# Sums of weight quarters in a down projection: by VectorE, or by DMAs that add in SBUF

## The chip, the cores and the metric

The kernel runs on one core of one Trainium2 chip. The metric is the device time of one execution in microseconds; the times shown are of several runs, and one further execution was recorded by the hardware profiler. Its instructions, DMAs and waits make the trace, and times in the trace count from its first instruction.

## The reference

One layer of a diffusion backbone: modulated input, one combined projection for two groups of attention heads, attention, output projection with gated residual and layer norm, and then the part that matters here, a gated feed-forward network with the same residual rule. All arrays are float32.

```python
SEQ = 256; D_MODEL = 2048; FFN_HIDDEN = 5632
def swiglu(u, w_gate, w_up, w_down):
    return (jax.nn.silu(u @ w_gate) * (u @ w_up)) @ w_down
...
x = layer_norm(DN_ALPHA * x + g2 * swiglu(modulate(x, sh2, sc2), w_gate, w_up, w_down), ln2_g, ln2_b)
```

The down projection is the last product: 256 tokens by 5632 hidden values, times a 5632 x 2048 weight.

## The kernel before, in words

Float32 accuracy is made of three products. Every operand is split in two: `hi` is the value rounded to the matmul's format (a cast on ScalarE, L236 or L230) and `lo` is what is left (a subtraction on VectorE, L237 or L231). `mm3` (L239 and the lines after it) then issues three matmuls for one 128 x 512 tile, hi by hi (L240), hi by lo (L241) and lo by hi (L242).

Weights are loaded by SP's queue (L208) as 1 MB tiles called `raw`, in four buffers. A buffer goes to a later load as soon as all that reads or writes it is done. The split parts lie in tiles `hi` and `lo` of 128 x 1024, four buffers of each, used in turn: the fifth split waits until TensorE is done with the first.

**The down projection.** The hidden dimension is cut into 11 blocks f of 512, the output columns into 4 groups n of 512, and groups are done in pairs (n, n + 1) by `pair`. There are two kinds of blocks:

- Eight whole blocks, `plain`. Each is loaded and split once per column group: f0 to f7 for group n, s0 to s7 for group n + 1 in what follows. One such step loads 1 MB, makes two splits and issues 24 matmuls (2 halves of the tokens, 4 slices of 128 hidden values, 3 matmuls).
- Three blocks with half products, `by_quarters`, for f = 8, 9, 10. They do both column groups at once by a scheme of seven half products in place of eight. The weight of 512 x 1024 is taken as quarters b11, b12 (in the first load, `r1`) and b21, b22 (in the second, `r2`); the activations likewise, with sums s1 to s4 made by `quarter_sums`. The seven products are called b, p1, a, p7, p5, p6 and c; each has one split and 6 matmuls. Four of them need sums of weight quarters. These are four subtractions or additions of 128 x 1024 on VectorE (L1759), between the splits; two go in place, into `raw`, and two into the tile `sums`.

**What sets the order.** The call order is written by `ORDER`: f0 f1 8 f2 f3 9 f4 f5 f6 10 f7, then s0 to s7. A block with half products stands there as one piece: two loads, seven splits with the four sums between them, 42 matmuls. The scheduler then arranges each engine's list by readiness; TensorE keeps the call order. `turn()` counts calls and starts, at fixed counts, the steps that turn the last hidden block's activations and build the sums of blocks 8 to 10. After the products of a pair `combine_parts` and `first_block` add them up, gate them and add them to the residual; `l2_loads` (two 1 MB loads on SP) and `rows_of_last_norm` (two fills and twelve small DMAs on GpSimd) prepare the last norm.

GpSimd has nothing else to do in the down projection.

Of the kernel before, what the change touches and what calls it, by code (L numbers as in the profile page):

```python
# [163 lines left out]
def dit_layer(ctx: ExitStack, tc: tile.TileContext, x, c, cx, c_ctx, w_ada, b_ada, w_in, q_norm_g,  # L164
# [1573 lines left out]
    def by_quarters(f, n, bank, begins, ends):  # L1738
        r1, r2 = (load_raw(w_down, f * 4 + k, 2, n * NB, 2 * NB).rearrange("p (k n) -> p k n", k=2) for k in (0, 2))
        (b11, b12), (b21, b22) = ([r[:, :, :NB], r[:, :, NB:]] for r in (r1, r2))  # L1740
        x1, x2 = (room["x"][:, i].rearrange("p (k n) -> p k n", k=2) for i in range(2))
        h = [(c[f][:, 0:2, :P], c[f][:, 2:4, :P], c[f][:, 2:4, P:]) for c in (hTh, hTl)]
        q = quarters[f]
        lefts = {n: [h[c][i] for c in range(2)] for i, n in enumerate(("a11", "a12", "a22"))}
        lefts.update({f"s{i + 1}": [q[c][:, i] for c in range(2)] for i in range(4)})
        sub, add = ALU.subtract, ALU.add
        for name, left, right, after in (
            ("p1", "a11", b11, (x1, b22, b12, sub)),
            ("b", "s4", b22, (b12, b12, b11, sub)),
            ("a", "a12", b21, (x2, x1, b11, add)),  # L1750
            ("p7", "s3", x1, (b21, b21, x2, sub)),
            ("p5", "s1", b12, None),
            ("p6", "s2", x2, None),
            ("c", "a22", b21, None),
        ):
            hi, lo = (whl.tile([P, SUB * NB], F32R, tag=tag, name=tag).rearrange("p (k n) -> p k n", k=2) for tag in ("hi", "lo"))
            split(hi, lo, right)
            if after:
                nc.vector.tensor_tensor(after[0], after[1], after[2], op=after[3])  # L1759
# [182 lines left out]
```

## Time and profile before

| What | Value |
|---|---|
| Median of 3 runs | 1115.16 us (1114.07 to 1115.31) |
| Profiled execution, its own time | 1115.46 us |
| Its span, first to last instruction | 1113.6 us |
| TensorE busy (modelled ends) | 1100.1 us |
| VectorE busy | 899.3 us |
| Granted clock of TensorE, mean | 0.997 |
| First matmul of the down projection | at 870.23 us |
| Its last | at 1102.76 us |

In the profile PE is TensorE's matmuls and PEld its weight loads, DVE is VectorE, ACT ScalarE, POOL GpSimd, SP the engine that issues most DMAs; SPq is its queue. A row of the order of time has start, duration, engine, line, operation, operands, and in brackets how long the engine stood idle before it and who ended that. Since matmuls overlap, the distance from one start to the next says how fast TensorE goes, not the 0.39 us of each.

### The profile page before, as it was taken

Reading aid. Unit: us, or ns where it says so; the run is one execution under the profiler, and the core shown is the slowest. Engines: PE = TensorE matmul, PEld = TensorE weight load, DVE = VectorE, ACT = ScalarE, POOL = GpSimd, SP = SyncE. Lnnn points to the kernel's source line nnn. Section 1 sums busy time; section 2 is a strip of 40 time slices with the busy share of each in tenths; the row PEclk is TensorE's granted clock in tenths of the full one; section 3 lists DMA queues with packets and bytes.
Section 4 is the critical chain, followed back from the end, with each engine's and each line's share of the span. In section 5 each row is a group of like instructions: output and inputs, shape, how many; then the busy total and the mean of one; then the engine's idle time right before and its main releaser. Section 6 shows DMA issues by size and latency. Waiting matters only on the chain.

```text
span 1113.6 us, 13934 instructions
## 1 busy us (share of the span) xinstructions
PE 1100.1 (99%) x5138; PEld 888.5 (80%) x5138; DVE 899.3 (81%) x1082; ACT 603.6 (54%) x870; POOL 48.5 (4%) x100
## 2 busy tenths in 40 slices
PE   8999999999999999999999999999999999999997
PEld 6677788778878788888888888888888788888886
DVE  2469999999989898877666776887875899678895
ACT  3345675786765356444465455655654565346550
POOL 1000050102000010000000000000000000001000
PEclk9999999999999999999999999999999999999999
DMA  9999998889999789989757898898896576546661
GB/s 344 374 401 393 396 337 323 300 274 312 328 317 366 278 314 359 336 288 346 269 207 279 288 323 286 304 309 306 310 317 216 164 249 226 192 151 224 222 236 76
DMA packets 175658, 321.28 MB, mean 288 GB/s; under 512 B 9283, under 2 KB 47075, under 8 KB 173285
## 3 DMA queue, kind: packets, MB, share of 16 engines
q1 hardware_dynamic: 173718, 319.23, 81.3%
q10 hardware_dynamic: 1264, 1.11, 0.3%
q8 instruction: 40, 0.66, 0.2%
q14 instruction: 28, 0.23, 0.1%
q0 software_dynamic: 608, 0.06, 0.0%
HBM read 304.11 MB, written 16.25 MB: 288 GB/s over the span
## 4 chain that ended last, share of the span: by engine, by line
PE 92%; DMA 3%; DVE 3%; ACT 1%; issue 0%; SPq 0%; ACTq 0%; DVEq 0%
PE acc L240 22%; PE acc L242 22%; PE acc L241 22%; PE wk L242 7%; PE wk L241 7%; PE wk L240 7%; PE wk L558 2%; PE wk L1036 2%; DMA raw<-in_w_ada_dram 2%; DVE adav L359 1%; DMA pT<-pd 1%; PE wk L728 1%; DMA adav<-in_b_ada_dram 0%; DVE lo L237 0%; DMA pd<-hx 0%
## 5 line engine op out<-in xcount | busy, mean ns | idle before, releaser
L231 DVE TENSOR_TENSOR lo<-raw,hi 128x1024 fp32r<-128x1024 f32 x232 | 280.9, 1221 | 126.8 <-ACT hi L230 124.0
L230 ACT CAST hi<-raw 128x1024 fp32r<-128x1024 f32 x232 | 244.0, 1056 | 245.3 <-PE acc L242 140.1
L240 PE MATMUL acc<-hi,u2h 128*128 128x512 f32 x448 | 175.1, 391 | 0.0
L242 PE MATMUL acc<-hi,u2l 128*128 128x512 f32 x448 | 174.6, 390 | 0.2 <-DVE u2l L1574 0.2
L241 PE MATMUL acc<-lo,u2h 128*128 128x512 f32 x448 | 174.5, 389 | 0.0
L359 DVE SCALAR_TENSOR_TENSOR adav<-raw,cs,adav 128x1024 f32<-128x1024 f32 (+1 forms) x96 | 114.4, 1191 | 6.1 <-DMA raw<-in_w_ada_dram 2.9
L507 ACT CAST hi<-raw 128x1024 fp32r<-128x1024 f32 x84 | 87.7, 1052 | 55.9 <-PE acc L242 28.7
L510 DVE TENSOR_TENSOR lo<-raw,hi 128x1024 fp32r<-128x1024 f32 x84 | 101.2, 1220 | 9.9 <-ACT hi L507 9.7
L240 PE MATMUL acc<-hi,hTh 128*128 128x512 f32 x264 | 102.6, 389 | 0.6 <-ACT hi L236 0.6
L240 PE MATMUL acc<-hi,uh 128*128 128x512 f32 x256 | 102.8, 402 | 0.3 <-ACT uh L741 0.3
L241 PE MATMUL acc<-lo,hTh 128*128 128x512 f32 x264 | 102.7, 389 | 0.0
L242 PE MATMUL acc<-hi,hTl 128*128 128x512 f32 x264 | 102.5, 389 | 0.0
L242 PE MATMUL acc<-hi,ul 128*128 128x512 f32 x256 | 100.3, 392 | 0.0
L241 PE MATMUL acc<-lo,uh 128*128 128x512 f32 x256 | 99.8, 390 | 0.0
L242 PE MATMUL wk<-hi,u2l 128*128 128x512 f32 x256 | 99.6, 389 | 0.0
L241 PE MATMUL wk<-lo,u2h 128*128 128x512 f32 x256 | 99.6, 389 | 0.0
L240 PE MATMUL wk<-hi,u2h 128*128 128x512 f32 x256 | 99.6, 389 | 0.0
L240 PEld LDWEIGHTS acc<-hi,u2h 128*128 128x128 f32 x448 | 84.1, 188 | 18.1 <-ACT u2h L1573 0.8
L242 PEld LDWEIGHTS acc<-hi,u2l 128*128 128x128 f32 x448 | 84.1, 188 | 18.1 <-DVE u2l L1574 0.6
L241 PEld LDWEIGHTS acc<-lo,u2h 128*128 128x128 f32 x448 | 84.1, 188 | 17.7 <-DVE lo L231 0.4
L240 PEld LDWEIGHTS acc<-hi,uh 128*128 128x128 f32 x256 | 48.1, 188 | 16.1 <-ACT acc L522 2.5
L240 PEld LDWEIGHTS acc<-hi,hTh 128*128 128x128 f32 x264 | 49.6, 188 | 11.4 <-ACT hi L236 1.0
(328 smaller groups left out, 1753.2 us busy)
## 6 DMA issues: line engine op xcount, KB each, us to landing
raw<-in_w_ada_dram SPq DMA_DIRECT2D x64, 1024.0 KB, 7.3
raw<-in_w_gate_dram SPq DMA_DIRECT2D x44, 1024.0 KB, 6.0
raw<-in_w_up_dram SPq DMA_DIRECT2D x44, 1024.0 KB, 5.7
raw<-in_w_down_dram SPq DMA_DIRECT2D x44, 1024.0 KB, 5.9
raw<-in_w_ada_dram SPq DMA_DIRECT2D x64, 512.0 KB, 6.3
raw<-in_w_in_dram SPq DMA_DIRECT2D x18, 1024.0 KB, 8.5
raw<-in_w_out_dram SPq DMA_DIRECT2D x16, 1024.0 KB, 6.4
pd<-hx SPq DMA_DIRECT2D x64, 128.0 KB, 4.7
```

The costliest lines, as they stand in the source:

```text
L230: nc.scalar.copy(hi[:, :n], raw[:, s : s + n])
L231: nc.vector.tensor_tensor(lo[:, :n], raw[:, s : s + n], hi[:, :n].bitcast(F32), op=ALU.subtract)
L240: nc.tensor.matmul(ps, lhsT=xh, rhs=w[0], start=first, stop=False, skip_group_check=seeded)
L241: nc.tensor.matmul(ps, lhsT=xh, rhs=w[1], start=False, stop=False, skip_group_check=seeded)
L242: nc.tensor.matmul(ps, lhsT=xl, rhs=w[0], start=False, stop=last, skip_group_check=seeded)
L359: nc.vector.scalar_tensor_tensor(a[:, c : c + piece], raw[:, f : f + piece], cs[:, 4 * (g * (G4 * NB // w) + j) + 2, None], a[:, c : c + p ...
L507: nc.scalar.copy(hl.hi[:, :n], raw.t[:, s : s + n])
L510: nc.vector.tensor_tensor(hl.lo[:, :n], raw.t[:, s : s + n], hl.hi[:, :n].bitcast(F32), op=ALU.subtract)
L558: nc.tensor.matmul(bank.t[32 * j : 32 * j + 32, :width], lhsT=cs[:, 4 * k + 2 - 2 * i : 4 * k + 34 - 2 * i], rhs=raw.t[:, c * width : (c + ...
L728: nc.tensor.transpose(ps.t[:, (j * 2 + t) * P : (j * 2 + t + 1) * P], src, ident)
L1036: nc.tensor.matmul(o_ps.t[:, : 2 * P].rearrange("p (g q) -> p g q", q=32), lhsT=v, rhs=pv[:, k], start=k == 0, stop=k == 3)
```

## The change

The four sums of weight quarters are made by DMAs that add: GpSimd issues a DMA from one quarter to another, in SBUF, with an addition at the destination (`put_on`). There is only an addition, so the signs are turned: quarters add up where they were subtracted, the activation sums s1 to s4 are subtracted the other way round, p1, a and c come out negative, and the copy of p1 and the two sums of `first_block` take that back.

A block becomes three pieces. Piece a (8a) makes both loads and the products b, p1 and a, and issues the four adding DMAs: 1, b22 += b12; 2, b12 += b11; 3, b11 += b22; 4, b21 += b11. Piece b does p7 (on the new b22) and p5 (b12), piece c does p6 (b11) and c (b21). A whole step stands between the pieces. `l2_loads` and `rows_of_last_norm` are called after s2 of the second pair.

```diff
 QUARTERS = {8: (9, 13), 9: (10, 11), 10: (9, 9)}
-ORDER = (0, 1, 8, 2, 3, 9, 4, 5, 6, 10, 7)
+ORDER_WORDS = "f0 f1 8a f2 8b f3 8c f4 9a f5 9b f6 9c f7 10a s0 10b s1 10c s2 C s3 A s4 s5 s6 s7"
+TWO_LATE = 20
...
-        for o, x0, x1, op in ((s1, a21, a22, ALU.add), (s2, s1, a11, ALU.subtract), (s3, a11, a21, ALU.subtract),
-                              (s4, a12, s2, ALU.subtract)):
-            nc.vector.tensor_tensor(o, x0, x1, op=op)
+        for o, x0, x1 in ((s1, a21, a22), (s2, a11, s1), (s3, a21, a11), (s4, a12, s2)):
+            nc.vector.tensor_tensor(o, x0, x1, op=ALU.subtract)
...
     def by_quarters(f, n, bank, begins, ends):
...
-        for name, left, right, after in (
-            ("p1", "a11", b11, (x1, b22, b12, sub)),
-            ("b", "s4", b22, (b12, b12, b11, sub)),
-            ("a", "a12", b21, (x2, x1, b11, add)),
-            ("p7", "s3", x1, (b21, b21, x2, sub)),
-            ("p5", "s1", b12, None),
-            ("p6", "s2", x2, None),
-            ("c", "a22", b21, None),
-        ):
...
-            if after:
-                nc.vector.tensor_tensor(after[0], after[1], after[2], op=after[3])
...
+        def put_on(right, other):
+            nc.gpsimd.dma_start(st[right], st[other], accum_op=ALU.add)
+
+        def one():
+            loads()
+            product("b", "s4", "b22")
+            put_on("b22", "b12")
+            product("p1", "a11", "b11")
+            put_on("b12", "b11")
+            put_on("b11", "b22")
+            product("a", "a12", "b21")
+            put_on("b21", "b11")
+            turn()
+
+        def two():
+            product("p7", "s3", "b22")
+            product("p5", "s1", "b12")
+
+        def three():
+            product("p6", "s2", "b11")
+            product("c", "a22", "b21")
+            turn()
+
+        return one, two, three
...
-            nc.scalar.copy(c1, banks["p1"])
+            nc.scalar.activation(c1, banks["p1"], AF.Copy, scale=-1.0)
...
-                nc.vector.tensor_add(y, banks["ac"[t]], y)
+                nc.vector.tensor_sub(y, banks["ac"[t]], y)
...
-    run(two[0][2:])
-    second_start(0, 3, two[5])
-    two[2]()
+    run(two[2:TWO_LATE])
     l2_loads()
     rows_of_last_norm()
-    run(two[1][1:3])
-    two[3]()
-    run(two[1][3:-4])
+    run(two[TWO_LATE:-4])
```

On VectorE, at block 8 of the first pair, this stood before (`lo` is the second half of a split, `sums` and `raw` on L1759 the sums of weight quarters):

```order
L1463 STREAM_TRANSPOSE hx<-hh 128x4x4x32 x2
L237 TENSOR_TENSOR lo<-raw,hi 128x1024
L1759 TENSOR_TENSOR sums<-raw 128x1024
L237 TENSOR_TENSOR lo<-raw,hi 128x1024
L1759 TENSOR_TENSOR raw<-raw 128x2x512
L237 TENSOR_TENSOR lo<-raw,hi 128x1024
L1759 TENSOR_TENSOR sums<-sums,raw 128x1024
L237 TENSOR_TENSOR lo<-sums,hi 128x1024
L1759 TENSOR_TENSOR raw<-raw,sums 128x2x512
L237 TENSOR_TENSOR lo<-raw,hi 128x1024
L237 TENSOR_TENSOR lo<-sums,hi 128x1024
L237 TENSOR_TENSOR lo<-raw,hi 128x1024
```

and this stands there now (L1498 are the sums of block 9's activations, L232 a split of a whole step, here f2):

```order
L1464 STREAM_TRANSPOSE hx<-hh 128x4x4x32 x2
L238 TENSOR_TENSOR lo<-raw,hi 128x1024 x2
L1498 TENSOR_TENSOR sums<-spill 128x256 x2
L1498 TENSOR_TENSOR sums<-spill,sums 128x256
L238 TENSOR_TENSOR lo<-raw,hi 128x1024
L1498 TENSOR_TENSOR sums<-spill,sums 128x256
L232 TENSOR_TENSOR lo<-raw,hi 128x1024 x2
L238 TENSOR_TENSOR quarters<-sums,quarters 128x1024
```

The four sums are gone from the list, the first split of the block keeps its place behind the transposes, and after three splits of block 8 come those of f2.

On GpSimd, with what each instruction waits for, the four adding DMAs of block 8 and the first of block 9 (`raw_7544` and `raw_7546` are block 8's first and second load, `raw_7745` and `raw_7747` block 9's; DMASW7, 0, 1 and 2 are the semaphores that adding DMAs 1, 2, 3 and 4 of block 8 raise, DMAHW those of SP's DMAs, DVE that of VectorE):

```order
L1759 DMA raw_7546<-raw_7544 128x2x512 [waits DMAHW4_49,DMAHW3_49,DMAHW5_49,DMAHW2_49,DMAHW6_49,DMAHW1_49,DMAHW7_49,DMAHW0_49,DVE_49]
L1759 DMA raw_7544<-raw_7544 128x2x512 [waits DMAHW5_49,DMAHW7_49,DMAHW1_49,DMASW7_49]
L1759 DMA raw_7544<-raw_7546 128x2x512 [waits DMASW0_49,DVE_49]
L1759 DMA raw_7546<-raw_7544 128x2x512 [waits DMASW1_49,DVE_49]
L1759 DMA raw_7747<-raw_7745 128x2x512 [waits DMAHW2_49,DMAHW3_49,DMASW2_49,DVE_49]
```

All of these are new; each waits for the one before it.

On SP, with waits, the loads at block 9 of the first pair before (`raw_7711` and `raw_7713` are block 9's):

```order
L208 DMA raw_7711<-in_w_down_dram 128x2x1024 [waits DVE_49]
L208 DMA raw_7713<-in_w_down_dram 128x2x1024 [waits DVE_49]
L208 DMA raw_7793<-in_w_down_dram 128x4x512 [waits DVE_49]
L208 DMA raw_7839<-in_w_down_dram 128x4x512 [waits DVE_49,Activation_49]
L208 DMA raw_7873<-in_w_down_dram 128x4x512 [waits DMAHW1_49,DVE_49]
```

and now, from f4's load to that of f6:

```order
L209 DMA raw_7711<-in_w_down_dram 128x4x512 [waits DMAHW7_49,DVE_49]
L1474 DMA hf_7783<-hd_7701 128x512 [waits DMAHW1_49,DMAHW2_49,DMAHW0_49,PE_49]
L1474 DMA hf_7785<-hd_7706 128x512 [waits DMAHW5_49,DMAHW4_49,DMAHW6_49,DMAHW3_49,PE_49]
L209 DMA raw_7745<-in_w_down_dram 128x2x1024 [waits DVE_49]
L209 DMA raw_7747<-in_w_down_dram 128x2x1024 [waits DMASW1_49,DMASW2_49,DMASW0_49,DVE_49]
L209 DMA raw_7787<-in_w_down_dram 128x4x512 [waits DMASW7_49,DVE_49]
L209 DMA raw_7853<-in_w_down_dram 128x4x512 [waits DMAHW7_49,DVE_49]
```

The load of f4 now stands ahead of block 9's, and block 9's second load takes the buffer of block 8's first: it waits for adding DMAs 2, 3 and 4 and, on VectorE, for the split of p6. Block 10's second load stands in the same way behind block 9.

More of the change, by code (lines that the diff above doesn't have):

```diff
@@ L1738, in by_quarters @@
     def by_quarters(f, n, bank, begins, ends):
[L1739 to L1744, printed above, removed]
@@ new lines, in loads @@
+        def loads():
+            h = [(c[f][:, 0:2, :P], c[f][:, 2:4, :P], c[f][:, 2:4, P:]) for c in (hTh, hTl)]
+            r1, r2 = (load_raw(w_down, f * 4 + k, 2, n * NB, 2 * NB).rearrange("p (k n) -> p k n", k=2) for k in (0, 2))
+            for i, r in enumerate((r1, r2)):
+                for j in range(2):
+                    st[f"b{i + 1}{j + 1}"] = r[:, :, j * NB : (j + 1) * NB]
+            q = quarters[f]
+            st.update({a: [h[c][i] for c in range(2)] for i, a in enumerate(("a11", "a12", "a22"))})
+            st.update({f"s{i + 1}": [q[c][:, i] for c in range(2)] for i in range(4)})
@@ L1756, in by_quarters, with product @@
+        def product(name, left, right):
             hi, lo = (whl.tile([P, SUB * NB], F32R, tag=tag, name=tag).rearrange("p (k n) -> p k n", k=2) for tag in ("hi", "lo"))
-            split(hi, lo, right)
-            if after:
-                nc.vector.tensor_tensor(after[0], after[1], after[2], op=after[3])
-            own = len(name) == 2
+            split(hi, lo, st[right])
             for j in range(2):
-                mm3(bank(name), lefts[left][0][:, j], lefts[left][1][:, j], (hi[:, j], lo[:, j]),
-                    j == 0 and begins(name), j == 1 and own and ends)
@@ L1812, in second_block @@
                 spread(t, n + 1)
-        return [first(f) for f in ORDER], [second(f) for f in whole], combine_parts, first_block, second_block, bank, whole
+        words = {"C": combine_parts, "A": first_block}
+        for f in whole:
+            words[f"f{f}"], words[f"s{f}"] = first(f), second(f)
+        for f in parts:
+            words.update(zip((f"{f}a", f"{f}b", f"{f}c"), by_quarters(f, n, bank, begins, f == parts[-1])))
+        return [words[w] for w in ORDER_WORDS.split()], second_block, bank, whole
     def second_start(f, n, bank):
@@ L1820, in second_start @@
         turn()
-    one = pair(0)
-    run(one[0])
-    second_start(0, 1, one[5])
-    one[2]()
-    run(one[1][1:3])
-    one[3]()
-    run(one[1][3:])
-    two = pair(2, 1)
-    run(two[0][:2])
-    one[4]()
-    run(two[0][2:])
-    second_start(0, 3, two[5])
-    two[2]()
+    one, one_end, _, _ = pair(0)
+    run(one)
+    two, two_end, two_bank, two_whole = pair(2, 1)
+    run(two[:2])
+    one_end()
+    run(two[2:TWO_LATE])
     l2_loads()
     rows_of_last_norm()
-    run(two[1][1:3])
-    two[3]()
-    run(two[1][3:-4])
+    run(two[TWO_LATE:-4])
     wide = pb.tile([P, 2, 2, SUB * NB], F32R, tag="u2h", name="wide")
@@ L1868, in dit_layer @@
         ending(0)
[L1869 removed]
+        gated(1, 3, two_bank("d"), t2k("yt"))
         nc.vector.tensor_add(xt[:, 1, cols[3]], xt[:, 1, cols[3]], ends[1])
```

24 lines of the change are left out of this document (11 added, 13 removed).

## The prediction

> **What bounds the kernel now.** I read the page first, then the windows of the down projection, then the order of time on TensorE and VectorE there, and last the DMA answers. The page's first lines:
>
> ```profile
> span 1113.6 us, 13934 instructions
> PE 1100.1 (99%) x5138; PEld 888.5 (80%) x5138; DVE 899.3 (81%) x1082; ACT 603.6 (54%) x870; POOL 48.5 (4%) x100
> ```
>
> TensorE is the bound, but a modelled end hides short holes, so I count matmuls by stretch. The windows (PE, PEld, DVE, ACT, POOL busy, then clock, DMA share, GB/s):
>
> ```profile
> 860.00:880.00 20.00, 20.00 (x90) 16.53 (x89) 14.47 (x18) 8.83 (x10) 0.00 (x0) 1.00 0.56 191
> 880.00:900.00 20.00, 19.35 (x83) 15.06 (x82) 20.00 (x22) 13.48 (x14) 0.00 (x0) 1.00 0.66 211
> 900.00:920.00 20.00, 20.00 (x90) 16.57 (x89) 19.96 (x22) 12.64 (x12) 0.00 (x0) 1.00 0.62 218
> ```
>
> Where VectorE is full (20.00 of 20 us) TensorE starts 83 matmuls instead of 90; beside it VectorE is just as full and TensorE loses nothing. The loss is one place, the first block with half products. What the weight loads of TensorE waited for there:
>
> ```profile
> 885.85 0.19 PEld L240 LDWEIGHTS wk<-hi,quarters 128*128 128x128 f32 x1 [0.46 <-ACT hi L236]
> 888.11 0.19 PEld L240 LDWEIGHTS acc<-hi,hTh 128*128 128x128 f32 x1 [1.04 <-ACT hi L236]
> 892.51 0.19 PEld L241 LDWEIGHTS acc<-lo,hTh 128*128 128x128 f32 x1 [0.43 <-DVE lo L231]
> ```
>
> Now the whole down projection, by its first matmul, the thirteenth, and its last:
>
> ```profile
> 870.23 0.39 PE L240 MATMUL acc<-hi,hTh 128*128 128x512 f32 x1
> 872.95 0.39 PE L240 MATMUL acc<-hi,hTh 128*128 128x512 f32 x1
> 1102.76 0.39 PE L242 MATMUL wk<-hilo,hTl 128*128 128x512 f32 x1
> ```
>
> Twelve matmuls take 2.72 us, 0.2267 us each. A pair of column groups has 8 whole blocks of 2 x 24 matmuls and 3 blocks of 42, so 510; two pairs have 1020, before and after alike. Their 1019 steps need 231.0 us and took 232.5. So all that VectorE's load costs TensorE here is 1.5 us, which is 0.14% of the time; I take 0.2% (2.2 us) as what a measurement of this kernel can tell from no change.
>
> **What is taken away.** The four additions of weight quarters per block, on VectorE:
>
> ```profile
> L1759 DVE TENSOR_TENSOR sums<-raw x6: 1214/1216/1226, 878.9 to 1034.9; 128x1024 f32<-128x1024 f32 x6
> L1759 DVE TENSOR_TENSOR sums<-sums,raw x6: 1210/1217/1219, 883.4 to 1038.3; 128x1024 f32<-128x1024 f32 x6
> L1759 DVE TENSOR_TENSOR raw<-raw,sums x6: 1215/1224/1226, 885.7 to 1045.7; 128x1024 f32<-128x1024 f32 x6
> ```
>
> With the fourth form, 24 additions of 1.22 us: 29 us less on VectorE. Of that at most the 1.5 us is on the path. I take all of it as won: **minus 1.5 us**. The turned signs cost nothing: the subtractions of activation quarters, the two of the first column group and the copy with a factor on ScalarE have the same sizes as what they replace, on engines that stay under TensorE's load.
>
> **What is added: a chain of four DMAs per block.** Each addition becomes a DMA of 128 x 1024 floats (524 KB) that GpSimd issues, and each waits for the one before: 2 overwrites what 1 reads, 3 reads what 1 wrote and overwrites what 2 reads, 4 reads what 3 wrote. Call one such DMA's time, from its wait being over to its landing, L. No row of before shows one. The nearest rows: the landing of GpSimd's plain DMAs of 2 to 4 KB (the two groups of them), GpSimd's own start behind a fill, the fastest stretch of plain loads, and the first and last of four stretches in a row, within such a block, in which no DMA runs.
>
> ```profile
> L342 POOL DMA_DIRECT2D adav<-in_b_ada_dram x7: 487/497/743, 382.5 to 539.8; - x7
> DMA to landing us min/median/max: 2.7/5.0/5.3
> L1720 POOL DMA_DIRECT2D rows<-in_ln_b_dram x6: 487/487/487, 1009.8 to 1031.6; - x6
> DMA to landing us min/median/max: 4.1/5.2/5.8
> 1009.25 0.53 POOL L1720 DMA_DIRECT2D rows<-in_ln_g_dram  x1 [0.29 <-POOL rows L1717]
> 1052.00:1054.00 2.00, 2.00 (x10) 1.68 (x9) 2.00 (x3) 1.62 (x2) 0.00 (x0) 1.00 1.10 432
> 1042.00:1044.00 2.00, 2.00 (x10) 1.67 (x9) 0.55 (x1) 0.65 (x1) 0.00 (x0) 1.00 0.00 0
> 1048.00:1050.00 2.00, 2.00 (x11) 1.65 (x10) 2.00 (x3) 1.61 (x2) 0.00 (x0) 1.00 0.00 0
> ```
>
> At 432 GB/s one pass of 524 KB takes 1.2 us. From below: the quickest small DMA and one pass, 2.7 + 1.2 = 3.9 us. From above: the slowest and two passes (an addition reads both operands), 5.8 + 2.4 = 8.2 us. I take 0.3 for the start, 2.7 for the quickest DMA, since the queue stands idle for long stretches of a block (0.00 of it busy from 1042 to 1050), and two passes: **L = 5.4 us**.
>
> The Trainium skill's page "DMA: Bandwidth & Descriptors" (Anatomy of one DMA — SWDGE (gpsimd) path) fits such DMAs by about 2.0 us plus bytes at 436 GB/s, and "Collectives: The Full Stack" (The bandwidth ceiling: the fold count and why AG ≠ RS ≠ AR) halves the rate of an addition for its two reads: an estimate of 4.4 us by both pages. The small DMAs above, with next to no bytes, took 2.7 to 5.8 us, so this trace is above that constant; no run here yet shows the rate of an addition.
>
> **Where L meets the path.** The durations of a split, of a weight load, and the first split of a block with half products beside its first matmul:
>
> ```profile
> L231 DVE TENSOR_TENSOR lo<-raw,hi 128x1024 fp32r<-128x1024 f32 x232 | 280.9, 1221 | 126.8 <-ACT hi L230 124.0
> L230 ACT CAST hi<-raw 128x1024 fp32r<-128x1024 f32 x232 | 244.0, 1056 | 245.3 <-PE acc L242 140.1
> L208 SPq DMA_DIRECT2D raw<-in_w_down_dram x44: 367/368/433, 845.0 to 1073.4; - x44
> DMA to landing us min/median/max: 5.0/5.9/12.2
> 877.78 1.18 DVE L237 TENSOR_TENSOR lo<-raw,hi 128x1024 fp32r<-128x1024 f32 x1
> 881.11 0.39 PE L240 MATMUL wk<-hi,hTh 128*128 128x512 f32 x1
> ```
>
> A split is 1.06 + 1.22 = 2.3 us, a load 5.5 us (between 5.0 and 5.9). A product is 6 matmuls, 1.36 us; a whole block 5.44; the pieces 8a, 8b, 8c take 4.08, 2.72 and 2.72, and with f2, f3, f4 between them 9a starts 25.84 us after 8a if nothing waits. Take the start of 8a as zero. The first split ended at 877.78 + 1.18, 2.1 us ahead of the block's first matmul, and the new order has a block's first split in the same place, so DMA 1 of block 8 can start at -2.1.
>
> Within a block the products are spread well: p7 wants DMA 1 and p5 DMA 2 some 9.5 and 10.9 us in. What binds lies behind DMA 4. The second load of block 9 goes into the buffer that held block 8's first load, so it waits on SP for DMAs 2, 3 and 4 (its row in the order above names them), and block 9's first split needs that load. From DMA 1 of one block to DMA 1 of the next this makes 4L, then a load, then a split: 4L + 5.5 + 2.3 = 4L + 7.8. Block 10's DMA 1 starts at -2.1 + 2 x (4L + 7.8), its last product c can start 4L + 2.3 later, at 12L + 15.8. TensorE gets to c of block 10 at 2 x 25.84 + 19.04 = 70.7 us. So a pair of column groups is late by 12L - 54.9 us, nothing up to L = 4.6. At 5.4 it is 9.9 us per pair; after 10c six whole blocks follow, which take no product from the chain, so each pair starts anew: **plus 19.8 us** for two.
>
> Queued behind the waits: on SP, behind the second load of block 9, the loads of f5 and f6, which TensorE needs a whole piece or more after 9a, hence no further price; on ScalarE and VectorE, behind the split of p5, those of the next whole block, which it needs after p5 anyway; on GpSimd only the next addition and, in the second pair, twelve small DMAs of 0.49 us, which it issues while an addition is under way. The row of the last norm's bias now loads ahead of f7, whose buffer comes free later; its gain row waits on SP for 10c, with the last two weight loads behind it. These are needed two whole blocks and two halves later, 16.3 us, and need about 5.9 + 2 x 2.4 us: nothing, and 2.4 us for each were that cover gone.
>
> **Sum.** The profiled execution took 1115.46 us, 0.3 above the median of the runs shown, 1115.16. 1115.46 - 1.5 + 19.8 = 1133.8 on its scale, 1133.5 on that of the median. **Forecast: 1133.5 us, slower**, as long as L is between 4.73 and 6.3; those ends give 2 x 1.9 - 1.5, about +2, and 2 x 20.7 - 1.5, about +40: its own range is 1117 to 1155.
>
> **Rivals.** *The additions are hidden.* With one pass instead of two L is 0.3 + 2.7 + 1.2 = 4.2 us; 12L - 54.9 is below zero, nothing is late, and the 1.5 us are won: 1113.7 us. It decides up to L = 4.73, where twice the lateness has eaten the gain and 2.2 us more. For it: the queue's idle stretches, and no row shows two passes. Against it: nothing but the quickest small DMA supports even 4.2. The estimate of 4.4 us from the pages above lands on this side too.
>
> *The additions are slowed by the loads beside them.* Inside the chain's 22 us run at least the loads of f4 and of block 9's first half, and the small DMAs beside loads took 4.1 to 5.8 us, not 2.7. At L = 7 a pair loses 29.1 us: 1115.2 - 1.5 + 58.2 = 1171.9. For it: those medians of 5.0 and 5.2. Against it: loads hold the queue for only some 2 x 2.4 us of each chain.
>
> *VectorE's relief helps elsewhere.* A gain over 2.2 us would need holes in TensorE's row that the 1.5 us do not contain; I find none, since nothing ahead of the down projection moves and the chain behind the last matmul is the same.
>
> **How the numbers follow.** The forecast's case 0.42, hidden 0.35, slowed by loads 0.20, more than 2.2 us won 0.03. So faster 0.03, same 0.35, slower 0.62. The range runs from 1113, below the hidden case, to 1160, which is L = 6.5 (2 x 23.1 - 1.5 = 44.7 over 1115.2); outside lie most of the third case and the last one, under 2 in 10.
>
> **What would show it.** Right: additions that land 5 to 6 us after GpSimd's wait ends; VectorE some 29 us less busy; TensorE whole through block 8, then waiting at the start of 9a or at p5, p6, c of blocks 9 and 10, released by a cast that itself waited for a DMA; SP's load behind DMA 4. Wrong: 90 matmuls in every 20 us of the down projection (then L is under 4.6 us), or waits in block 8 already, at p7 and p5 (then L is over 6 us), or late f2 and f3 instead of late products (then loads, not the chain, are the trouble).

## The result and the profile after

| Kernel | Median | Runs |
|---|---|---|
| before | 1114.62 us | 4 (1113.99 to 1115.31) |
| changed | 1174.11 us | 4 (1173.76 to 1176.73) |

The changed kernel is slower: the ratio is 1.0539, with a 95% interval of 1.0526 to 1.0551. The forecast of 1133.5 us had the sign and not the size, and its range ended at 1160. The first lines of the page of the changed kernel (lines of the code stand one number higher now: L241 to L243 are the three matmuls, L1759, where the sums on VectorE stood before, is now `put_on`):

```profile
span 1172.3 us, 13999 instructions
...
PE 1123.6 (96%) x5138; PEld 899.8 (77%) x5138; DVE 873.5 (75%) x1058; ACT 601.6 (51%) x870; POOL 78.4 (7%) x124
```

VectorE is relieved, by 25.8 us of the 29 expected (899.3 before; 24 instructions fewer). The windows of the same three stretches as before, with the columns as before:

```profile
860.00:880.00 20.00, 20.00 (x90) 16.57 (x89) 15.11 (x22) 9.38 (x11) 1.28 (x1) 1.00 0.56 180
880.00:900.00 20.00, 15.59 (x62) 12.26 (x61) 9.98 (x10) 8.53 (x10) 2.82 (x3) 0.91 0.76 168
900.00:920.00 20.00, 17.36 (x67) 12.88 (x66) 13.06 (x15) 9.56 (x10) 1.98 (x2) 0.91 0.85 269
```

From block 8 on TensorE starts 62 and 67 matmuls in 20 us instead of 90, VectorE and ScalarE are half idle, and there is something new: the granted clock is 0.91 in both stretches. The first matmul of the down projection, its last, and the first step of the end behind it:

```profile
868.77 0.39 PE L241 MATMUL acc<-hi,hTh 128*128 128x512 f32 x1
...
1158.21 0.39 PE L243 MATMUL wk<-hilo,hTl 128*128 128x512 f32 x1
1164.57 0.55 PE L1891 MATMUL wk<-ident,columns 128*66 128x128 f32 x2 [3.25 <-DVE columns L1890]
```

The down projection takes 289.4 us where its 1019 steps need 231.0: it loses 58.5 us, against 1.5 before. From the last matmul to the end of the span are 14.1 us (1172.3 - 1158.2) instead of 10.9 (1113.6 - 1102.8). It also began 1.5 us sooner in this execution (868.8 us; 868.4 to 869.9 in the runs below, 870.2 before). 58.5 - 1.5 + 3.2 - 1.5 = 58.7, the difference of the two spans: nothing was lost anywhere else.

GpSimd's starts of the four additions of block 8 and the first of block 9, then the group of all 24 with the times to landing:

```profile
877.79 1.28 POOL L1759 DMA_DIRECT2D raw<-raw  x1 [327.78 <-DMA hd<-hx]
885.62 1.22 POOL L1759 DMA_DIRECT2D raw<-raw  x1 [6.54 <-DMA raw<-raw]
893.84 1.19 POOL L1759 DMA_DIRECT2D raw<-raw  x1 [7.00 <-DMA raw<-raw]
899.59 1.21 POOL L1759 DMA_DIRECT2D raw<-raw  x1 [4.57 <-DMA raw<-raw]
914.48 1.18 POOL L1759 DMA_DIRECT2D raw<-raw  x1 [13.69 <-DVE lo L238]
```

```profile
L1759 POOL DMA_DIRECT2D raw<-raw x24: 1183/1212/1285, 877.8 to 1113.7; - x24
...
DMA to landing us min/median/max: 5.0/6.0/10.7
```

From start to start the additions take 7.8, 8.2 and 5.75 us, and block 9 begins 36.7 us behind block 8, where TensorE's work between them is 25.84. Over the six blocks the time from DMA 1's start to the cast on ScalarE that DMA 4's landing releases is 27.6 us on average, so L is 6.9 us, not 5.4. TensorE's weight loads that waited in block 8, and who waited for the additions in all:

```profile
894.34 0.19 PEld L241 LDWEIGHTS wk<-hi,quarters 128*128 128x128 f32 x1 [4.07 <-ACT hi L237]
...
906.78 0.19 PEld L241 LDWEIGHTS acc<-hi,hTh 128*128 128x128 f32 x1 [2.04 <-ACT hi L237]
```

```profile
ACT hi L237 <- DMA raw<-raw: 89.5, 20, 9.2
POOL raw L1759 <- DMA raw<-raw: 88.3, 15, 10.0
```

In the first fence the first row is p5, which wants DMA 2, and the second c, which wants DMA 4. In the second (waits in total, how often, the longest) ScalarE stood 89.5 us for additions, with the splits of later steps behind it. Block 8 itself is late already, at p5 and at c, though not at p7: most of the sign that the prediction had listed for an L over 6 us.

### The profile page after: what moved, and what is told of

Its sections match the earlier page's. It is cut to its first block, busy times and chain, and to the rows that moved or that the text cites. A ratio compares the mean times of both kernels' runs of the same rounds, so it can differ in the third digit from the quotient of the medians.

```text
span 1172.3 us, 13999 instructions
## 1 busy us (share of the span) xinstructions
PE 1123.6 (96%) x5138; PEld 899.8 (77%) x5138; DVE 873.5 (75%) x1058; ACT 601.6 (51%) x870; POOL 78.4 (7%) x124
## 5 line engine op out<-in xcount | busy, mean ns | idle before, releaser
L232 DVE TENSOR_TENSOR lo<-raw,hi 128x1024 fp32r<-128x1024 f32 x232 | 280.2, 1220 | 117.0 <-ACT hi L231 113.4
L231 ACT CAST hi<-raw 128x1024 fp32r<-128x1024 f32 x232 | 242.2, 1054 | 221.0 <-PE acc L243 123.0
L241 PE MATMUL acc<-hi,u2h 128*128 128x512 f32 x448 | 175.1, 391 | 0.0
L243 PE MATMUL acc<-hi,u2l 128*128 128x512 f32 x448 | 174.6, 390 | 0.6 <-DVE u2l L1574 0.6
L238 DVE TENSOR_TENSOR lo<-raw,hi 128x1024 fp32r<-128x1024 f32 x42 | 50.9, 1223 | 109.4 <-ACT hi L237 109.0
L241 PE MATMUL acc<-hi,hTh 128*128 128x512 f32 x264 | 108.9, 413 | 11.4 <-ACT hi L237 11.4
L508 ACT CAST hi<-raw 128x1024 fp32r<-128x1024 f32 x84 | 87.7, 1051 | 58.5 <-PE acc L243 35.1
L242 PE MATMUL acc<-lo,hTh 128*128 128x512 f32 x264 | 108.9, 412 | 4.9 <-DVE lo L238 4.0
L511 DVE TENSOR_TENSOR lo<-raw,hi 128x1024 fp32r<-128x1024 f32 x84 | 101.1, 1219 | 11.1 <-ACT hi L508 10.9
L237 ACT CAST hi<-raw 128x1024 fp32r<-128x1024 f32 x42 | 43.6, 1049 | 124.4 <-DMA raw<-raw 89.5
L243 PE MATMUL acc<-hi,hTl 128*128 128x512 f32 x264 | 107.2, 406 | 0.0
L241 PE MATMUL acc<-hi,uh 128*128 128x512 f32 x256 | 102.8, 402 | 0.3 <-ACT uh L742 0.3
L243 PE MATMUL acc<-hi,ul 128*128 128x512 f32 x256 | 100.3, 392 | 0.0
L243 PE MATMUL wk<-hi,u2l 128*128 128x512 f32 x256 | 99.6, 389 | 0.0
L241 PE MATMUL wk<-hi,u2h 128*128 128x512 f32 x256 | 99.6, 389 | 0.0
L243 PEld LDWEIGHTS acc<-hi,u2l 128*128 128x128 f32 x448 | 84.1, 188 | 18.5 <-DVE u2l L1574 1.0
L241 PEld LDWEIGHTS acc<-hi,u2h 128*128 128x128 f32 x448 | 84.1, 188 | 18.1 <-ACT u2h L1573 0.8
```

Source lines behind the costliest of these rows:

```text
L231: nc.scalar.copy(hi[:, :n], raw[:, s : s + n])
L232: nc.vector.tensor_tensor(lo[:, :n], raw[:, s : s + n], hi[:, :n].bitcast(F32), op=ALU.subtract)
L237: nc.scalar.copy(hi, src)
L238: nc.vector.tensor_tensor(lo, src, hi.bitcast(F32), op=ALU.subtract)
L241: nc.tensor.matmul(ps, lhsT=xh, rhs=w[0], start=first, stop=False, skip_group_check=seeded)
L242: nc.tensor.matmul(ps, lhsT=xh, rhs=w[1], start=False, stop=False, skip_group_check=seeded)
```

## The experiments

Twelve kernels, each the changed kernel with the edit shown. "Loses" means the time between the first and the last matmul of the down projection beyond 231.0 us. Where the text gives a wait of TensorE, it is counted from start to start, less the 0.23 us of one step; the brackets of TensorE's rows count from the modelled end of the matmul before and show some 0.2 us less.

| Run | Time (us) | Ratio to before, 95% | Loses (us) |
|---|---|---|---|
| no_sums | 1116.58 | 1.0024 (1.0014 to 1.0034) | 0.6 |
| no_sums_early_end | 1112.77 | 0.9988 (0.9979 to 0.9997) | 0.0 |
| vector_sums | 1122.34 | 1.0074 (1.0053 to 1.0095) | 7.1 |
| early_ends | 1174.58 | 1.0542 (1.0527 to 1.0558) | 58.2 |
| copies | 1148.60, one run | | 32.4 |
| light_loads | 1168.24, one run | | 52.1 |
| no_loads | 1151.49, one run | | 37.0 |
| zeros | 1168.13 | 1.0487 (1.0464 to 1.0509) | 52.2 |
| fifth_buffer | 1171.78, one run | | 56.3 |
| distance | 1173.35 | 1.0536 (1.0518 to 1.0553) | 51.5 |
| distance_inside | 1156.96 | 1.0382 (1.0366 to 1.0397) | 37.0 |
| two_by_dma | 1154.50 | 1.0354 (1.0322 to 1.0387) | 39.1 |

### The order without the chain: no_sums, no_sums_early_end, vector_sums, early_ends

```diff
         def put_on(right, other):
-            nc.gpsimd.dma_start(st[right], st[other], accum_op=ALU.add)
+            pass
```

> The order in three pieces, with neither adding DMAs nor sums on VectorE: the four sums of weight quarters are left out, the products take the quarters as loaded. Theory (the changed kernel's loss is the wait for the chain, plus 3 us at the end that the order brings): TensorE goes without a hole from the first to the last matmul of the down projection, the 1.5 us of before are won, the end is 14 us instead of 10.9: 1116 to 1118 us. Rival (the order in pieces, with its loads and splits, costs by itself what the run with the sums on VectorE lost in blocks 8 to 10, 5 us, or more): 1121 us or above.

1116.58 us. The windows of no_sums, its last matmul, and the columns behind it:

```profile
880.00:900.00 20.00, 20.00 (x90) 16.57 (x89) 17.03 (x20) 13.05 (x15) 0.00 (x0) 1.00 0.56 190
900.00:920.00 20.00, 20.00 (x90) 16.56 (x89) 13.90 (x13) 11.51 (x11) 0.00 (x0) 1.00 0.61 217
```

```profile
1100.81 0.39 PE L243 MATMUL wk<-hilo,hTl 128*128 128x512 f32 x1
1107.50 0.69 PE L1891 MATMUL wk<-ident,columns 128*66 128x128 f32 x2 [3.58 <-DVE columns L1890]
```

TensorE starts 90 matmuls in each stretch at full clock. All but 0.6 us of what the down projection loses is gone. So the pieces, the loads and the splits cost next to nothing, and the additions cost the rest. The end is 14.1 us long here too (span 1114.9), without any chain: it belongs to the order.

Then the same with the combining where it stood before:

```diff
-ORDER_WORDS = "f0 f1 8a f2 8b f3 8c f4 9a f5 9b f6 9c f7 10a s0 10b s1 10c s2 C s3 A s4 s5 s6 s7"
-TWO_LATE = 20
+ORDER_WORDS = "f0 f1 8a f2 8b f3 8c f4 9a f5 9b f6 9c f7 10a 10b 10c s0 C s1 s2 A s3 s4 s5 s6 s7"
+TWO_LATE = 19
```

> As the run without sums (the four sums are left out, the products take the quarters as loaded), but block 10's three pieces follow each other behind f7, the combining is called behind s0 and the sums of the first column group behind s2, as they stood before. Theory (the 3 us at the end come from block 10's last products and the combining, which stand a step or two nearer to the end, with VectorE busy behind them): the end is 11 us again, TensorE keeps its unbroken row, so 1112.5 to 1114 us: this is also the most that taking the sums off VectorE could ever win, whoever makes them. Rival (the longer end has another cause, the late row of the last norm or the last loads): 1116 to 1117 us, as the run without sums.

```profile
1100.11 0.39 PE L243 MATMUL wk<-hilo,hTl 128*128 128x512 f32 x1
1103.64 0.43 PE L1891 MATMUL wk<-ident,columns 128*66 128x128 f32 x2 [0.42 <-DVE columns L1890]
```

1112.77 us, and the columns come 3.5 us behind the last matmul, as before, instead of 6.7. In the changed order block 10's last product stands three whole steps nearer to the end than the block did, the combining two and the sums of the first column group one; VectorE is then behind with them when the last matmul is done. This run is also the bound: without any sums at all the whole idea is worth 1.5 us (0.3 to 2.3 by the interval of the ratio).

early_ends moved only the words C and A, in the changed kernel, one step forward ("10c C s2 A s3").

> As the changed kernel, but the combining of the half products and of the first column group's sums is called one whole step earlier (behind 10c and s2 instead of s2 and s3). Theory (the last matmul is followed by 14.1 us instead of 10.9 because the combining on VectorE now stands a step or two nearer to the end, whatever the chain does): the end is some 2 to 3 us shorter and the rest as it was: 1170 to 1173 us, with TensorE's wait ahead of the columns at 1 us or less. Rival (the longer end comes from late loads or splits of the last steps): no change, 1174 us.

1174.58 us, the rival's side: no change that could be told. The wait ahead of the columns was 2.2 us for 3.4, but the split of s2 now stood behind the combining and TensorE waited 2.5 us for it. So here moving the two words wins nothing.

In vector_sums VectorE makes the sums in place:

```diff
-            nc.gpsimd.dma_start(st[right], st[other], accum_op=ALU.add)
+            nc.vector.tensor_tensor(st[right], st[right], st[other], op=ALU.add)
```

> The new order in three pieces is kept, but the four sums of weight quarters are made by VectorE again, in place, with the turned signs; no adding DMA is left. Theory (the chain of adding DMAs is the whole loss): the chain is gone, the four 1.22 us sums are back on VectorE, which costs TensorE no more than the 1.5 us of before, so 1113 to 1118 us; the end behind the last matmul may stay some 3 us longer than before (14.1 us in the changed kernel, 10.9 before) if it is the order that made it so. Rival (the new order itself is late, loads or splits come in a worse sequence): well over 1120 us, with TensorE waiting in blocks 8 to 10 as in the changed kernel.

1122.34 us, above what was expected and at the edge of the rival's range. The first matmuls that waited in its block 8:

```profile
885.21 0.51 PE L241 MATMUL wk<-hi,quarters 128*128 128x512 f32 x1 [0.50 <-ACT hi L237]
886.96 0.50 PE L242 MATMUL acc<-lo,hTh 128*128 128x512 f32 x1 [1.25 <-DVE lo L232]
```

The second is f2, whose `lo` stands behind the four sums on VectorE. So VectorE's sums do cost TensorE in this order, 7.1 us in all, where the order of before kept that to 1.5. It speaks against the new order with sums on VectorE, not for the DMAs.

### What an addition takes: copies, light_loads, no_loads

```diff
-            nc.gpsimd.dma_start(st[right], st[other], accum_op=ALU.add)
+            nc.gpsimd.dma_start(st[right], st[other])
```

> The adding DMAs become plain copies of the same size from and to the same places, issued by GpSimd with the same waits; the additions themselves are left out. In the changed kernel an adding DMA with nothing beside it moves its first bytes 1.8 us after its start, its last 4.7 us after, and the next one starts 5.65 us after it. Theory (the addition reads both operands, so it moves at half the rate): about 1.5 us of the 2.9 us of moving go, L is 4.2 us alone and perhaps 5 with the loads beside it; by 12L - 54.9 a pair is late by 0 to 7 us, so 1113 to 1128 us. Rival (the rate is that of GpSimd's queue, or of its many small pieces, whatever the DMA does): L stays at 5.65 us and more, and the time near 1172.

GpSimd's starts in block 8 of the second pair, and a window in which one copy alone moves; then the window of an addition alone, DMA 3 of block 8 in the changed kernel (the last three columns are the clock, the share of the 16 DMA engines, GB/s):

```profile
1011.77 0.72 POOL L1759 DMA_DIRECT2D raw<-raw  x1 [50.33 <-DVE lo L238]
1015.29 0.72 POOL L1759 DMA_DIRECT2D raw<-raw  x1 [2.79 <-DMA raw<-raw]
1019.05 0.73 POOL L1759 DMA_DIRECT2D raw<-raw  x1 [3.04 <-DMA raw<-raw]
1024.00 0.72 POOL L1759 DMA_DIRECT2D raw<-raw  x1 [4.22 <-DMA raw<-raw]
```

```profile
925.48:927.00 1.52, 1.05 (x3) 0.83 (x3) 1.52 (x3) 1.10 (x2) 0.00 (x0) 0.50 0.90 345
```

```profile
895.50:898.50 3.00, 2.90 (x7) 2.32 (x8) 2.92 (x4) 1.21 (x2) 0.00 (x0) 0.50 1.02 175
```

By the trace's DMA packets an addition with nothing beside it has its first bytes 1.76 us after its start, moves for 2.92 us, and the next one starts 0.96 us later: 5.65 us. A copy has 1.30, 1.50 and the same 0.96: 3.76 us. Moving takes twice as long for an addition. So the forecast's two passes have the right size; that the second is a read of the second operand, no row shows. The Trainium skill's page "Collectives: The Full Stack" (The bandwidth ceiling: the fold count and why AG ≠ RS ≠ AR) halves the rate for the addition of a ReduceScatter, because it reads two sources; these 1.50 and 2.92 us agree with the half.

The time, 1148.60 us, is far above the 1113 to 1128 expected, and below the rival's 1172. Here too the copies beside loads take more (up to 8.3 us from start to start), and the estimate went by the wrong link, as the runs with the distances show below.

light_loads takes three quarters of the weights of f2 to f7 off the queue:

```diff
-        w = load_split(w_down, f * 4, n * NB)
+        if f < 2 or f > 7 or n % 2:
+            w = load_split(w_down, f * 4, n * NB)
+        else:
+            one = load_raw(w_down, f * 4, 1, n * NB, NB)[:, None, :].to_broadcast([P, SUB, NB])
...
```

> The whole steps f2 to f7 load only the first quarter of their weights (256 KB for 1 MB) and use it four times; three quarters of these weights are left out of the result. Splits, matmuls and adding DMAs stay. Theory (loads beside the additions lengthen them from 5.65 to 6.5 to 11 us): most additions now take 5.65 us, the blocks follow one another every 4 x 5.65 + 8.8 = 31.4 us instead of 37, and a pair loses 13 to 15 us instead of some 29: 1139 to 1147 us. Rival (the long additions are slow for a reason of their own, not for the loads): they stay at a mean of 7 us and the time within 5 us of 1172.

1168.24 us: by the time the rival's side, within 5 us of 1172, but the additions did not stay as they were. One shows the effect. DMA 1 of block 9, which took 11.15 us in the changed kernel, takes 5.40:

```profile
914.11 1.18 POOL L1767 DMA_DIRECT2D raw<-raw  x1 [16.06 <-DVE lo L238]
919.51 1.20 POOL L1767 DMA_DIRECT2D raw<-raw  x1 [4.21 <-DMA raw<-raw]
```

By the DMA packets 2.5 MB of loads moved beside it before and 0.3 MB now. But each of the six DMAs 4 still had about 1 MB beside it, as in the changed kernel: the blocks' own loads, 1 MB each, were left whole. So the edit had not taken away all that it was meant to. The six chains, from DMA 1's start to DMA 4's landing, are 6.2 us shorter in all, and the down projection loses 6.4 us less.

no_loads does: f2 to f7 use a half tile that is loaded once per pair.

```diff
-        w = load_split(w_down, f * 4, n * NB)
+        if f < 2 or f > 7 or n % 2:
+            w = load_split(w_down, f * 4, n * NB)
+        else:
+            kept = room["x"][:, 1]
+            if f == 2:
+                nc.sync.dma_start(kept.rearrange("p (k n) -> p k n", k=2),
+                                  w_down[f * 4 * P : (f * 4 + 2) * P, n * NB : (n + 1) * NB].rearrange("(k p) n -> p k n", p=P))
+            w = split_raw(kept) + split_raw(kept)
```

> The whole steps f2 to f7 make no load at all: they split a half tile that is loaded once per pair and use it twice (the result leaves out their own weights). Splits, matmuls, adding DMAs and the loads of the blocks with half products stay. By the eleven kernels so far a block is late by the time from its DMA 1's start to its DMA 4's landing + 0.2 - 19.04 us, and 1 to 3 us more for the slow clock behind a hole. Theory (1 MB that is loaded beside an addition makes it some 2 us longer): with at most one load beside a chain 4L falls from 28 to between 22.0 and 24 us, most additions take 5.65 to 5.9 us, a block is late by 4 to 8 us instead of 9.7: 1142 to 1165 us. Rival (the long additions are not the loads' doing): L stays at a mean of 7 us, 1170 or more.

1151.49 us, as expected. Block 9 in the first pair and the first addition of block 10:

```profile
912.38 1.18 POOL L1766 DMA_DIRECT2D raw<-raw  x1 [12.70 <-DVE lo L238]
917.74 1.20 POOL L1766 DMA_DIRECT2D raw<-raw  x1 [4.18 <-DMA raw<-raw]
923.68 1.19 POOL L1766 DMA_DIRECT2D raw<-raw  x1 [4.73 <-issue]
929.35 1.21 POOL L1766 DMA_DIRECT2D raw<-raw  x1 [4.48 <-issue]
940.60 1.19 POOL L1766 DMA_DIRECT2D raw<-raw  x1 [10.04 <-DVE lo L238]
```

5.4, 5.9 and 5.7 us, and 28.2 us from block to block instead of 37.0. Where loads are left, in block 10 of the second pair with 1.4 and 1.0 MB beside its first two, additions still take 7.5 and 9.6. That the loads lengthen the additions is shown, and taking these loads away is worth 21.5 of the 58.5 us even though the blocks' own loads stayed. In that are the chains, 17.1 us shorter in all, and the clock, which is at half for 17 us instead of 41. That DMAs started by different engines share the same 16 DMA engines is also what the Trainium skill says on "DMA: Bandwidth & Descriptors" (Issuing engines are not separate DMA queues).

### Which link holds TensorE: fifth_buffer, distance, distance_inside

fifth_buffer takes block 9's second load, in the second pair, out of its wait for DMAs 2 to 4 of block 8.

```diff
-    def load_raw(w, k0, nk, c0, width):
-        raw = raw_tile()
+    def load_raw(w, k0, nk, c0, width, fifth=False):
+        raw = pb.tile([P, G4 * NB], F32, tag="u2l1", name="raw") if fifth else raw_tile()
...
+            r1, r2 = (load_raw(w_down, f * 4 + k, 2, n * NB, 2 * NB, f == 9 and n == 2 and k == 2).rearrange("p (k n) -> p k n", k=2)
+                      for k in (0, 2))
```

> In the second pair of column groups alone, block 9's second load goes into a room of its own (the one that later holds a row of the last norm), so it no longer waits for DMAs 2, 3 and 4 of block 8, and block 10's loads find buffers that are free earlier. The first pair is as in the changed kernel and serves as the comparison. Theory (load behind DMA 4, then split, is the 8.8 us in each chain from block to block): the second pair's blocks follow one another after 4L alone, 26 to 28 us at L = 6.5 to 7 instead of 32.3 and 34.1; its lateness falls from 26 to between 7 and 14 us, the first pair's stays at 32: 1154 to 1163 us. Rival (GpSimd's queue alone sets the pace, the load is hidden beside it): the second pair's distances stay above 31 us and the time within 4 us of 1174.

Its additions of blocks 8 and 9 in the second pair, and the first of block 10:

```profile
1022.16 1.19 POOL L1760 DMA_DIRECT2D raw<-raw  x1 [49.14 <-DVE lo L238]
...
1040.15 1.21 POOL L1760 DMA_DIRECT2D raw<-raw  x1 [4.47 <-DMA raw<-raw]
1052.44 1.19 POOL L1760 DMA_DIRECT2D raw<-raw  x1 [0.26 <-issue]
1060.81 1.26 POOL L1760 DMA_DIRECT2D raw<-raw  x1 [6.11 <-issue]
1070.17 1.26 POOL L1760 DMA_DIRECT2D raw<-raw  x1 [7.07 <-DMA raw<-raw]
...
1088.15 1.22 POOL L1760 DMA_DIRECT2D raw<-raw  x1 [0.66 <-DVE lo L238]
```

1171.78 us: in the time the rival's side. From block to block 30.3 and 35.7 us, together 66.0, against 32.3 and 34.1, together 66.4, in the changed kernel. The load that no longer waits lets DMA 1 of block 9 start 2 us sooner, and then moves beside the additions: the first two take 8.4 and 9.4 us, against 6.5 and 7.9. So the link that the forecast was built on, DMA 4, load, split, is not what holds the pace by itself, at the one block where it was taken away.

distance sets the blocks further apart, by steps of both column groups:

```diff
-ORDER_WORDS = "f0 f1 8a f2 8b f3 8c f4 9a f5 9b f6 9c f7 10a s0 10b s1 10c s2 C s3 A s4 s5 s6 s7"
-TWO_LATE = 20
+ORDER_WORDS = ("f0 f1 8a f2 f3 8b f4 8c f5 f6 9a f7 s0 9b s1 9c s2 s3 10a s4 s5 10b s6 10c C s7 A",
+               "f0 f1 8a f2 f3 8b f4 8c f5 9a f6 f7 9b s0 9c s1 10a s2 10b s3 10c C A s4 s5 s6 s7")
+TWO_LATE = 18
...
```

> All four sums stay adding DMAs; the blocks are set further apart by whole steps of both column groups between the pieces: 36.7 us from 8a to 9a and from 9a to 10a in the first pair, 31.3 us in the second (its last four whole steps are written apart and cannot be moved). Theory (the chain needs 4L + 8.8 = 32 to 37 us per block and costs only what TensorE's work between the pieces does not cover): the first pair is late by 0 to 5 us instead of 32, the second by 12L + 17.8 - 81.6, 4 to 20 us: 1121 to 1142 us, likeliest 1128. Rival (the additions hurt by themselves, by contention with the loads or by holding GpSimd): over 1150 us.

1173.35 us, the rival's side: the theory failed, though the first pair lost 19.3 us instead of 32.1. The traces name the link. DMA 1 of a block waits for the split of b, and ScalarE and VectorE can make splits only four tiles ahead of TensorE. So a chain starts 1.9 to 3.9 us ahead of its own block's start in the changed kernel, and no sooner where the block stands further off (here between 3.9 us ahead and 0.8 us behind). What must cover it is the work inside the block, from the start of a to product c: 19.04 us in the changed kernel. For block 8 of the changed kernel, the start of a and the cast that DMA 4 releases:

```profile
879.65 0.39 PE L241 MATMUL acc<-hi,quarters 128*128 128x512 f32 x1
...
905.69 1.04 ACT L237 CAST hi<-raw 128x1024 fp32r<-128x1024 f32 x1 [5.18 <-DMA raw<-raw]
```

From DMA 1's start at 877.79 to that cast are 27.9 us, less 1.9 of head start, and 2.3 for the split, less 19.04: 9.3 us late. Summed in this way over the six blocks it is 47.2 of the 58.5 us. TensorE's row agrees: 46.1 us are lost between the first matmul of a and the second of c, and 12.3 behind c. Of these 12.3, 9.4 are steps at half the clock (below); most of the rest are waits for the split of a whole step, which stands behind the late ones.

In the run distance c stood 24.5 us in (in block 10 of the second pair still 19.04), and the rest went to longer chains (29 us, with 3.4 MB of loads beside a chain instead of 3.1), to the slow clock behind the holes, and to the end, where TensorE waited 7.5 us for the columns.

distance_inside therefore moves the pieces of one block apart, two whole steps between each in the first pair, and keeps the blocks close:

```diff
+ORDER_WORDS = ("f0 f1 8a f2 f3 8b f4 f5 8c f6 9a f7 s0 9b s1 s2 9c 10a s3 s4 10b s5 s6 10c s7 C A",
+               "f0 f1 8a f2 f3 8b f4 f5 8c 9a f6 f7 9b s0 9c 10a s1 s2 10b s3 10c C A s4 s5 s6 s7")
+TWO_LATE = 23
...
```

> All four sums stay adding DMAs, loads stay. Now the pieces of one block are set apart, not the blocks: two whole steps between its pieces a and b and two between b and c in the first pair and in block 8 of the second (29.9 us from the start of a to c, instead of 19.04), two and one in blocks 9 and 10 of the second (24.5 us); the rows of the last norm are called at the end. Theory (each block's own chain is late for its own product c, 4L + 0.2 against 19.04; what lies between the blocks does not matter): at 4L = 27 to 31 us the first pair is late by 0 to 5 us, blocks 9 and 10 of the second by 3 to 7 each and 2.8 for the slow clock; with 3 to 7 us at the end 1127 to 1146 us, likeliest 1135. Rival (distance does not help, since more loads then meet the chain and lengthen it by as much, as in the run with the blocks set apart): over 1155 us.

1156.96 us: by the time just on the rival's side, but the first pair does what was expected. Its first matmul, and the first of the second pair 510 matmuls later:

```profile
869.17 0.39 PE L242 MATMUL acc<-hi,hTh 128*128 128x512 f32 x1
...
991.95 0.39 PE L242 MATMUL acc<-hi,hTh 128*128 128x512 f32 x1
```

These 122.8 us are 7.2 more than 510 steps need; in the changed kernel the first pair lost 32.1. The chains are as long as ever (27 to 30 us). So the link inside the block is shown there. The second pair loses 29.8, more than expected; 2.0 of it stands in its first step, behind the end of the first pair. ScalarE's waits there between 1060 and 1105 us:

```profile
ACT hi L238 <- DMA raw<-raw: 17.6, 3, 8.4
ACT rows L1723 <- DMA rows<-in_ln_b_dram: 10.7, 2, 5.7
```

The rows of the last norm come by small DMAs that GpSimd issues; twice one of them stood behind an addition that was waiting for the addition before it, and ScalarE, which copies the rows, waited for it, 10.7 us in all, with the casts of the splits that follow behind it. The combining is at the very end here and TensorE waits 7.7 us for the columns.

### Half the additions: two_by_dma

```diff
-            nc.gpsimd.dma_start(st[right], st[other], accum_op=ALU.add)
+            if right in ("b22", "b12"):
+                nc.gpsimd.dma_start(st[right], st[other], accum_op=ALU.add)
+            else:
+                nc.vector.tensor_tensor(st[right], st[right], st[other], op=ALU.add)
```

> The order in three pieces stays; only b22 += b12 and b12 += b11 are adding DMAs, and VectorE makes the other two sums in place. Theory (a chain that comes to more than 25.84 us per block is the loss): the chain is 2L + 2 x 1.2 + 8.8, 22.5 to 25.2 us at L = 5.65 to 7, hidden; what is left is the order's own cost (the run with all four sums on VectorE took 7.7 us more than before, 3.3 us of it behind the last matmul), with half of VectorE's load taken off again: 1115 to 1122 us. Rival (each adding DMA costs its share whatever the chain's length): half the loss stays, some 1145 us.

1154.50 us (1148.29 to 1157.62), nearer to the rival's 1145 than to the theory. VectorE's two longest waits in blocks 9 and 10 of the first pair:

```profile
926.54 1.23 DVE L1762 TENSOR_TENSOR raw<-raw 128x1024 f32<-128x1024 f32 x1 [9.85 <-DMA raw<-raw]
...
960.41 1.23 DVE L1762 TENSOR_TENSOR raw<-raw 128x1024 f32<-128x1024 f32 x1 [9.96 <-DMA raw<-raw]
```

VectorE's own sum waits for a DMA, and all that is listed behind it waits too, p7's `lo` among it: TensorE waits 6.4 and 6.5 us there. The wait has moved from ScalarE to VectorE.

### The slow clock: zeros

```diff
...
             split(hi, lo, st[right])
+            for i in range({"p7": 16, "p6": 8}.get(name, 0)):
+                nc.tensor.matmul(bank("b"), lhsT=zeros, rhs=hTh[f][:, 0:2, :].rearrange("p a b -> p (a b)"),
+                                 start=False, stop=False)
```

> Ahead of p7 sixteen, and ahead of p6 eight matmuls of a tile of zeros are added into a bank that is open anyway, so that TensorE works (3.6 and 1.8 us) while it waits for the chain; the result stays the same. They should keep the granted clock at 1.00, where the changed kernel shows 41 us at 0.50 and 15.9 us of matmul starts lost to that. Theory (the chain sets when p7, p6 and c can go, so what the slow clock costs between them is hidden in a shorter wait): only what lies behind the last wait of a pair comes back, some 2 and 4 us, so 1166 to 1171 us. Rival (the slow clock adds up with the waits): 1155 to 1160 us. If the zeros only lengthen TensorE's work: 1174 or more.

```profile
880.00:900.00 20.00, 19.24 (x85) 15.42 (x84) 11.67 (x14) 8.10 (x9) 2.70 (x3) 1.00 0.76 170
900.00:920.00 20.00, 18.07 (x79) 14.43 (x78) 12.38 (x12) 10.00 (x10) 2.09 (x2) 1.00 0.98 309
```

The windows show the clock at 1.00 (0.998 over the run, 0.979 in the changed kernel); their counts of matmuls include those of zeros. The time falls to 1168.13 us, by 6.0, within the range that was expected; the intervals of the two ratios do not overlap. In the changed kernel matmuls that followed each other at half speed lost some 16 us: 6.8 between a and c, where c had to wait for the chain anyway, and 9.4 behind c, where they are a loss of their own. What the clock alone costs is not isolated by this run. The zeros are work themselves, 5.44 us per block, and where a block's chain was nearly covered they made it later (block 8 of the second pair: c 5.4 us late instead of 2.5); and in the profiled execution the six chains are 9.2 us shorter in all. So the 6.0 us are a net figure.

## Why the prediction went wrong, point by point

- **TensorE bounds, and VectorE costs it only 1.5 us.** Right, and shown: with the sums left out and the old end the kernel takes 1112.77 us, 1.5 less than the 1114.24 of before beside it.
- **L = 5.4 us.** This step failed. Its parts were near for an addition alone: 1.76 to the first bytes and 2.92 of moving, 5.65 from start to start. But the mean was 6.9, and the forecast multiplies L by 24. In its own formula, 12 x 6.9 - 54.9 = 27.9 us per pair and 1115.2 - 1.5 + 55.8 = 1169.5: the size of L alone accounts for 36 of the 40.6 us missed. The case taken as undisturbed, since "the queue stands idle for long stretches of a block", was the exception: 5 of the 24 additions had less than 100 KB moving beside them. The prediction's own windows show the DMA engines 56 to 66% busy with loads. The sum over the DMA engines was never made. The run no_sums has the new order's loads and no additions; its three periods from block to block in the first pair (the last column but one is the share of the DMA engines):

```profile
880.13:905.97 25.84, 25.84 (x115) 21.40 (x114) 20.57 (x23) 16.02 (x17) 0.00 (x0) 1.00 0.67 234
905.97:931.81 25.84, 25.84 (x115) 21.40 (x114) 15.84 (x14) 13.62 (x13) 0.00 (x0) 1.00 0.65 238
931.81:957.65 25.84, 25.84 (x115) 21.40 (x114) 19.05 (x19) 14.09 (x14) 0.00 (x0) 1.00 0.61 212
```

Four additions, 2.92 us each of all 16 engines, need 11.7 us of a period of 25.84; by these windows some 8.5 to 10 of them are free. This is an estimate, but it leaves no room.

- **The rival "slowed by the loads beside them", L = 7: 1171.9 us, chance 0.20.** This is what happened. The reason given against it, that loads hold the queue for 2 x 2.4 us of each chain, was wrong: by the DMA packets 3.1 MB of loads move beside a chain on average, their packets take 6 to 12 us of the 16 engines, and 13 of the 24 additions had 900 KB or more moving beside them.
- **What binds lies behind DMA 4 (load, split, next block).** Not by itself: with that wait removed at one block the pace stayed. The chain is late for its own block's c, 4L + 2.3 less a head start of 3.0 on average against 19.04 us, and p5 of block 8, which the prediction held to be "spread well", was late too. The prediction looked at p7 and p5 there and not at the same block's c, though its own numbers had it late: 4 x 5.4 + 2.3 - 2.1 is 21.8 us against 19.04, so TensorE could not stay "whole through block 8" even at L = 5.4. Three blocks make 12L - 59 per pair, not far from the forecast's 12L - 54.9; so the wrong link gave nearly the right number by luck, and the wrong idea of how to mend it.
- **Queued behind the waits: no price.** Nearly right in the changed kernel: behind c, all waits that are not steps at half the clock come to 2.6 us. In distance_inside and two_by_dma it was large, as soon as something else waited for a DMA on ScalarE or VectorE.
- **The end is the same.** Wrong by 3.2 us. The instructions were the same, but their last input, c of block 10, came later in the call order, and so did the combining.
- **The clock.** Not thought of. 9.4 us of steps at half speed lie behind c; holding the clock up with zeros won 6.0 us net, and what the clock alone is worth stays open.

By TensorE's row, on the scale of the spans: 1113.6 - 1.5 - 1.5 (the sooner start) + 46.1 (inside the blocks) + 12.3 (behind c) + 3.2 (the end) = 1172.2 of 1172.3 us. The formula for a late c gives 47.2 for the 46.1.

None of these kernels with its sums in place beats before: 1112.77 us, with no sums at all, is the floor, 0.12% below before, and a chain of four adding DMAs has to hide 22 us or more per block.

## What to carry to other kernels

Before work is moved to DMAs, add up the DMA engines' time in the stretch where it will run, loads and new transfers together, and price a chain of DMAs at its length beside loads, not alone. A chain that starts when its own block starts must be covered by work inside that block; setting blocks further apart does not help if the start moves with them. Work that only takes load off an engine that holds nobody up is worth what that engine's waits cost, here 1.5 us of 1114.

## What the runs showed of the hardware

- An adding DMA within SBUF, 524 KB, moves at half the rate of a copy: 2.92 against 1.50 us. GpSimd itself is busy 1.21 us with issuing it, against 0.73 for the copy.
- Per 1 MB of loads beside it an addition took some 2 us longer (a straight line through the 24 additions of the changed kernel: 4.7 us to the last bytes, and 1.9 per MB; 2.0 in light_loads). Single ones lie far off it: with 0.9 to 1.1 MB beside them it took 5.3 to 9.9 us. Over half of the excess lies ahead of the first bytes, which came up to 5.5 us after the start, against 1.76 alone.
- In the down projection of the changed kernel TensorE's granted clock went to 0.50 for stretches of 3.4 or 6.8 us, nine times, always in a hole or just behind one. The Trainium skill's page "TensorE: Matmul & The Clock Gate" (Part 1: The HAM clock gate) gives windows of 3.4 us, which these lengths bear out; it asks for an idle window to slow down, but here holes of 1.8 and 1.0 us close together (from 905 to 908 us, slow from 908.8) were enough, while holes of 1.2 and 1.0 us from 979 to 982 us were not.
